# State-space stage of a hybrid trunk: the samples' state products in plain fp32 on four row groups, and the dense third bank in the shared four

## The chip, the cores and the metric

One Trainium2 chip, one core of it. The metric is the device time of one launch in microseconds (us). The kernel before takes 1957.69 us, the median of 3 runs (1957.03 to 1958.97).

## What is computed

One layer over two request groups with shared weights: a prompt of 1024 tokens and 8 samples of 16 tokens, 1152 tokens in all. Attention and a Mamba-2 state-space branch (SSD) are computed from one input projection and merged. What matters here is the state that the SSD branch leaves behind, cut from the reference:

```python
to_end = jnp.exp(a_cs[:, -1:] - a_cs)
h_new = h * jnp.exp(a_cs[:, -1])[..., None, None] + jnp.einsum('blgn,blgep->bgepn', bk, xdt * to_end[..., None])
```

For the samples the chunk is the sample's own 16 tokens, so the sum runs over 16 rows, for each of 8 samples, with B (`bk`, 16 x 128) on one side and the weighted x (16 x 128 for two heads) on the other. All 8 samples lie together on the 128 partitions, 16 rows each. TensorE contracts over partitions, so a product over one sample's 16 rows alone needs the other samples' rows set to zero, or left out.

## The kernel before

All dense projections are done in three fp32r products (L442, L443, L445: high weight by high x, high by low, low by high), accumulated in PSUM: for each block of 128 output channels three thirds of 384 tokens, each third 8 x 3 = 24 products. A third is here called a bank, since it fills one PSUM bank. The weights of a block are loaded as fp32 and split in two by ScalarE (L334, the high part) and VectorE (L335, the rest). Two blocks' split weights fit; the next pair of tiles is free only when the block before has finished its last product.

PSUM has eight banks: two for the dense banks (pool `d`, tiles of that name), two in one tile `s`, four shared ones in pool `g`, handed out in turn. In `dense` (L471) a block's first and second banks are `d`; the third, once attention is over, is the first half of an `s` tile.

The work beside the projections is written as generators. `run` steps the dense generator, and lets the others (urgent and paced ones) issue in between by a clock of estimated PE time (`yield 215`, `pause(1500)`). The tile framework then orders each engine's queue with its own timeline; that order is fixed in the program, and each engine executes its queue strictly in order. Some pieces are kept in program order (`late`).

The SSD stage goes over 16 pairs of heads p, in four groups of four pairs. For a group, `group_lat` (L1367) transposes B to token rows (L1384, copied out by ScalarE at L1385) and computes C times B (L1390, taken out by VectorE at L1392), all in `g` banks. For a pair, `prelude` (L1431) loads the decay rows `acs_d` by DMA (L1441), and ScalarE forms the decays from them (nine steps at L1453, an exponential at L1457; L1459 on VectorE multiplies by the masked C-B). The dense blocks of a pair are z (taken out by ScalarE at L1423, VectorE at L1424), the convolution's x (L1240, L1243, L1244 on ScalarE, then L1260 to L1270) and, for ten pairs, one merge gate (L1355, ScalarE). Then `main` (L1465): x is transposed (L1481) and weighted into `xd` and `xw` (L1485, VectorE), the chunk states are multiplied (L1526) and scanned (L1531, L1535), y is computed (L1553, L1560, both on column halves of the array; L1566), the carried states are added (L1573, L1578, L1579), and y is stored (L1588, L1590, L1591).

Last in a pair come the samples' states (L1594 to L1607). B and xw of the samples are split into a high and a low fp32r part, and laid out so that the 128 rows hold one half of the samples (64 rows) twice: high in one half of the partitions, low in the other (L1491 to L1508: ScalarE copies, VectorE differences). GpSimd makes four masked copies of x, `masked` (L1511), each for two samples of each half, with a mask of period four (`bmask4`). For each mask two products of 128 x 128 by 128 x 256 (B high, B low; L1598) are accumulated: four products in one `g` bank, twice per pair, with a pause between, and VectorE adds each bank to the state (L1607).

Of the kernel before, what the change touches and what calls it, by code (L numbers as in the profile page):

```python
# [7 lines left out]
F32 = mybir.dt.float32  # L8
# [4 lines left out]
P = 128  # L13
# [21 lines left out]
COLS = 53184  # L35
QCOLS = 1024
VCOLS = 6 * 1024
RCOLS = 16 * NT + 4 * 1024 + 1280 + 32
FCOLS = COLS - RCOLS - QCOLS - VCOLS
NQ = 3 * P  # L40

NQL = NQ + 32

C_ID, C_U, C_UB, C_ONE, C_BLK, C_BM, C_SEL, C_S4, C_BM4 = 0, 128, 256, 384, 512, 640, 648, 680, 712
NCONST = 716

PARAMS = [("norm_g", KT), ("b_ada", 24), ("conv_w", NCV * 4), ("conv_b", NCV), ("qk_g", 2), ("dskip", NPAIR),
          ("ssd_g", NPAIR), ("dt_bias", 32), ("a_log", 32)]
# [73 lines left out]
def trunk_kernel(ctx: ExitStack, tc: tile.TileContext, h):  # L122
# [55 lines left out]
    for n, w in PARAMS:  # L178
# [17 lines left out]
    bmask = cst[:, C_BM:C_BM + NB]  # L196
    sel = cst[:, C_SEL:C_SEL + 32]
    sel4 = cst[:, C_S4:C_S4 + 9]
    bmask4 = cst[:, C_BM4:C_BM4 + 4]

    H0 = 0
    W0 = H0 + 16 * NT
# [3 lines left out]
    L_ATT = arena.set_layout(Z0, [("Q", 1, 16 * P), ("T", 5, NT), ("S", 10, 640), ("U", 2, 640), ("K", 4, 512), ("q", 1, 256), ("d", 1, 256),  # L206
                                  ("k", 1, 128), ("p", 1, 128), ("n", 2, 36 + 3 * 16), ("t", 6, 14)])
    L_ATT["Z"] = L_ATT["T"][2:]
    L_SSD = arena.set_layout(Z0, [("X", 1, XW), ("R", 2, 1184), ("t", 8, 36), ("pad", 1, 576), ("T", 9, NT), ("Y", 1, 1184), ("H", 1, 1024),
                                  ("g", 3, G3)])  # L210
    L_HEAD = dict(L_SSD, T=[x for x in L_SSD["T"] if x[0] + x[1] <= Z0 + 7 * NT])
    L_START = arena.set_layout(Z0, [("T", 11, NT), ("ada", 5, 1024), ("e", 2, 256)])
    L_TAIL = arena.set_layout(Z0, [("T", 15, NT)])
# [4 lines left out]
    L_WA = rarena.set_layout(W0, [("w", 2, 1024)])  # L218
    L_QR = rarena.set_layout(W0 + 2 * 1024, [("q", 3, 1024)])
    L_Q = qarena.set_layout(0, [("q", 1, 1024)])  # L220
    L_ST = rarena.set_layout(W0 + 4 * 1024, [("b", 4, P), ("s", 2, P), ("x", 2, 2 * P)])
    L_W3 = varena.set_layout(0, [("w", 2, 3 * 1024)])
    L_W7 = varena.set_layout(0, [("w", 2, 7 * NQL)])
    L_QS = qarena.set_layout(0, [("ada", 1, 1024)])
# [4 lines left out]
    def alloc(lay, tag, cols, cold=None):  # L229
        if lay is L_Q:  # L230
            try:
                return alloc(L_QR, tag, cols)
            except NoSlot:
                pass
        if lay is L_SSD and tag == "H":
            try:
                return Buf(qarena, qarena.alloc(L_QS, "ada", cols), cols)
            except NoSlot:
                pass
        if lay is L_Q or lay is L_QS:  # L240
# [3 lines left out]
        if lay is L_H or lay is L_W or lay is L_WA or lay is L_QR or lay is L_ST:  # L244
# [182 lines left out]
    def dense(ops, evict, nk=KT, outs=1, last=False, wide=False, order=(0, 1, 2), other=False):  # L427

        i = widx[0]
        widx[0] += 1
        hi, lo = yield from w_wait(i)
        if len(jobs[min(i + 1, len(jobs) - 1)]) > 3:
            w_next(i)

        def mm(ps, o, g, k, parts=(0, 1)):
            tok = slice(g * G3, (g + 1) * G3)
            wc = slice((k * outs + o) * P, (k * outs + o + 1) * P)
            kh, kl = ops[k]  # L440
            if 0 in parts:
                nc.tensor.matmul(ps, hi.r[:, wc], kh.r[:, tok], start=k == 0, stop=False)  # L442
                nc.tensor.matmul(ps, hi.r[:, wc], kl.r[:, tok], start=False, stop=False)  # L443
            if 1 in parts:
                nc.tensor.matmul(ps, lo.r[:, wc], kh.r[:, tok], start=False, stop=k == nk - 1)  # L445

        for o in range(outs):
            if wide or (last and o == outs - 1):
                if wide or other:
                    acc = [pg(G3) for _ in range(3)]  # L450
                else:
                    sp = pss.tile([P, 2, 512], F32, tag="s", name=nm("s"))
                    acc = [psd.tile([P, G3], F32, tag="d", name=nm("d")) for _ in range(2)] + [sp[:, 0, :G3]]
                for k in range(nk):
                    while len(ops) <= k:
                        blocked[0] = "operand"
                        yield None
                    for g in range(3):
                        mm(acc[g], o, g, k)
                        if k == nk - 1:  # L460
                            yield from evict(o, g, slice(g * G3, (g + 1) * G3), acc[g]) or ()
                        yield 3 * 162.5
                    if last and o == outs - 1:
                        for x in ops[k]:
                            x.free()
                    if k == 2 and o == 0:
                        w_next(i)
                continue
            for g in order:
                if g == 2 and att_left[0] == 0:  # L470
                    ps = pss.tile([P, 2, 512], F32, tag="s", name=nm("s"))[:, 0, :G3]  # L471
                else:
                    ps = psd.tile([P, G3], F32, tag="d", name=nm("d"))
                for k in range(nk):
                    while len(ops) <= k:
                        blocked[0] = "operand"
                        yield None
                    mm(ps, o, g, k)
                    if nk == KT and g == order[-1] and k in (3, 5, 7):
                        w_over(i, k)  # L480
                    yield 3 * 162.5
# [880 lines left out]
    grp = {}  # L1362

    def group_dense(g, lay):
        res = grp[g] = {"b": [], "c": [], "sq": None, "st": None}
        yield from conv_gen(16 + g, lay, res["b"])
        yield from conv_gen(20 + g, lay, res["c"])  # L1367

# [31 lines left out]
    def ssd(p):  # L1400
# [62 lines left out]
        def main():  # L1463
# [24 lines left out]
            me, eb, h0, tm = st["me"]  # L1488
            ssd_all[p + 1] = True

            if res["st"] is None:  # L1491
                bs = res["st"] = []
                for j in range(2):
                    rw, ro = slice(64 * j, 64 * j + 64), slice(64 - 64 * j, 128 - 64 * j)
                    b_ = tokb.ap[rw, NP:]
                    hi = yield from walloc(L_ST, "b", P)
                    lo = yield from walloc(L_ST, "b", P)
                    nc.scalar.activation(hi.r[rw], b_, AF.Copy)
                    nc.scalar.activation(hi.r[ro], b_, AF.Copy)
                    nc.vector.tensor_tensor(lo.r[rw], b_, hi.ap[rw], ALU.subtract)  # L1500
                    nc.vector.tensor_tensor(lo.r[ro], b_, hi.ap[rw], ALU.subtract)
                    bs.append((hi, lo))
            xs = []
            for j in range(2):
                rw, ro = slice(64 * j, 64 * j + 64), slice(64 - 64 * j, 128 - 64 * j)
                t = yield from walloc(L_ST, "s", P)
                nc.scalar.activation(t.r[rw], xw.ap[rw, NP:], AF.Copy)
                nc.vector.tensor_tensor(t.r[ro], xw.ap[rw, NP:], t.ap[rw], ALU.subtract)  # L1508
                xs.append(t)

            def masked(q):  # L1511

                t = alloc(L_ST, "x", 2 * P)
                i = 2 * (q % 2)
                nc.gpsimd.tensor_tensor(t.r.rearrange("p (b n) -> p b n", n=P), xs[q // 2].ap.unsqueeze(1).to_broadcast([P, 2, P]),
                                        bmask4[:, i:i + 2].unsqueeze(2).to_broadcast([P, 2, P]), ALU.mult)
                return t

            xm = [masked(0), masked(1)]

            yield from pause(1500)
            for j in range(2):
# [68 lines left out]
            nc.scalar.activation(z.ap, x.ap, AF.Square)  # L1591
            stored(x)
            yield from pause(2000)
            pss_ = [pg(), pg()]  # L1594
            for q in range(4):
                j, i = q // 2, q % 2
                for w, b_ in enumerate(res["st"][j]):
                    nc.tensor.matmul(pss_[j][:, 2 * i * P:2 * (i + 1) * P], b_.r, xm[q].r, start=w == 0, stop=w == 1)  # L1598
                xm[q].free()
                if q < 2:  # L1600
                    xm.append(masked(q + 2))
                yield 215
                if q == 1:
                    yield from pause(4500)
                if i:
                    c = slice(4 * j * P, (4 * j + 4) * P)
                    nc.vector.tensor_tensor(h0.ap[:, c], h0.ap[:, c], pss_[j], ALU.add)  # L1607
            for t in xs + [xw]:
                t.free()
            if res["sq"] is None:  # L1610
                res["sq"] = z
            else:
# [4 lines left out]
            stored(h0)  # L1617
            if p % PPG == PPG - 1:
                s = res["sq"]
                for t in (tokb, res["cbm"], res["ct"], *res["st"][0], *res["st"][1]):  # L1620
# [304 lines left out]
```

## Time and profile before

| | |
|---|---|
| median of 3 runs | 1957.69 us |
| profiled execution, first to last instruction (span) | 1955.7 us |
| TensorE (PE) busy | 1938.3 us, 99% |
| VectorE (DVE) busy | 1168.5 us, 60% |
| ScalarE (ACT) busy | 776.4 us, 40% |
| GpSimd (POOL) busy | 323.5 us, 17% |
| granted TensorE clock | full in all 40 slices |

Of the profiled execution only the span is given; its time from outside isn't listed, so the span stands for it, 2.0 us under the median. A row of a timeline reads: start in us, length in us, engine, line, operation, output<-input, shape, number of instructions merged in the row, and in brackets the engine's idle time before it with what ended it. PE is TensorE's products, PEld its weight loads, SPq the queue that starts DMAs. A plain fp32 product appears as two records, an fp32r product as one. Attention runs until about 750 us, the SSD pairs from there to about 1520 us, the last projections after that.

### The profile page before, as it was taken

To read this page: it belongs to the slowest core of one execution; us is meant where nothing else is said; L and a number is where in the kernel's file an instruction comes from. 1 tells how busy PE (TensorE), PEld (TensorE's weight loads), DVE (VectorE), ACT (ScalarE), POOL (GpSimd) and SP (SyncE) were. 2 spreads that over 40 slices of the span, in tenths; PEclk is the share of its full clock that TensorE was granted. 3 is DMA by queue.
4 is the path that set the end of the run, shared out by engine and by line. 5 is a ranking of instruction groups with operands and counts; after the bars stand their busy time and mean duration, and the time that the engine had idled before them with its cause. 6 is when DMAs were issued, how large, how long until landed. Compare 5 with 4: busy or idle time off the path is not lost.

```text
span 1955.7 us, 35068 instructions
## 1 busy us (share of the span) xinstructions
PE 1938.3 (99%) x14091; PEld 1859.4 (95%) x14091; DVE 1168.5 (60%) x2441; ACT 776.4 (40%) x1589; POOL 323.5 (17%) x624
## 2 busy tenths in 40 slices
PE   7999999999999999999999999999999999999999
PEld 5999999899998999999999999999999999999999
DVE  7455555556555765757566666576674334777732
ACT  8444444445444557344454434345351301111200
POOL 0312213122131201212212221122212100000000
PEclk9999999999999999999999999999999999999999
DMA  9124244232432325433333333332337642331241
GB/s 367 60 81 131 86 132 131 90 122 88 131 112 96 112 88 160 128 112 110 95 132 129 106 103 114 117 118 91 117 118 291 234 140 92 104 104 56 86 143 52
DMA packets 81209, 238.62 MB, mean 122 GB/s; under 512 B 14284, under 2 KB 15320, under 8 KB 81048
## 3 DMA queue, kind: packets, MB, share of 16 engines
q1 hardware_dynamic: 72088, 207.74, 32.7%
q0 software_dynamic: 8960, 28.65, 3.8%
q8 instruction: 111, 1.82, 0.4%
q14 instruction: 50, 0.41, 0.1%
HBM read 192.70 MB, written 43.66 MB: 121 GB/s over the span
## 4 chain that ended last, share of the span: by engine, by line
PE 96%; DVE 1%; ACT 1%; DMA 1%; issue 0%; SPq 0%
PE d L442 13%; PE d L443 13%; PE d L445 13%; PE s L442 5%; PE s L445 5%; PE s L443 5%; PE d L508 5%; PE d L506 5%; PE d L507 5%; PE g L1043 3%; PE g L1066 3%; PE g L1553 2%; PE s L1122 2%; PE g L1526 1%; PE g L1573 1%; PE g L1122 1%
## 5 line engine op out<-in xcount | busy, mean ns | idle before, releaser
L442 PE MATMUL d<-rarena 128*128 128x384 f32 x1520 | 517.4, 340 | 0.3 <-ACT arena L1355 0.3
L445 PE MATMUL d<-rarena 128*128 128x384 f32 x1520 | 511.4, 336 | 0.0
L443 PE MATMUL d<-rarena 128*128 128x384 f32 x1520 | 511.0, 336 | 0.0
L442 PEld LDWEIGHTS d<-rarena 128*128 128x128 f32 x1520 | 285.6, 188 | 4.6 <-issue 2.3
L443 PEld LDWEIGHTS d<-rarena 128*128 128x128 f32 x1520 | 285.6, 188 | 2.8 <-issue 2.4
L445 PEld LDWEIGHTS d<-rarena 128*128 128x128 f32 x1520 | 285.5, 188 | 1.1 <-issue 0.9
L334 ACT ACTIVATE rarena<-arena 128x1024 fp32r<-128x1024 f32 x92 | 97.5, 1060 | 314.1 <-PE s L443 226.2
L442 PE MATMUL s<-rarena 128*128 128x384 f32 x640 | 216.7, 339 | 0.0
L443 PE MATMUL s<-rarena 128*128 128x384 f32 x640 | 214.2, 335 | 0.0
L445 PE MATMUL s<-rarena 128*128 128x384 f32 x640 | 214.1, 334 | 0.0
L508 PE MATMUL d<-va_att,rarena 128*128 128x384 f32 (+1 forms) x559 | 195.0, 349 | 0.0
L506 PE MATMUL d<-va_att,rarena 128*128 128x384 f32 (+1 forms) x559 | 193.9, 347 | 0.0
L507 PE MATMUL d<-va_att,rarena 128*128 128x384 f32 (+1 forms) x559 | 191.0, 342 | 0.0
L335 DVE TENSOR_TENSOR rarena<-arena,rarena 128x1024 fp32r<-128x1024 f32 x92 | 113.2, 1230 | 82.7 <-ACT rarena L334 82.4
L1031 ACT ACTIVATE arena<-arena 128x640 f32<-128x640 f32 (+2 forms) x144 | 101.4, 706 | 138.0 <-DVE arena L1140 99.7
L442 PEld LDWEIGHTS s<-rarena 128*128 128x128 f32 x640 | 120.3, 188 | 1.0 <-issue 1.0
L443 PEld LDWEIGHTS s<-rarena 128*128 128x128 f32 x640 | 120.3, 188 | 0.0
L445 PEld LDWEIGHTS s<-rarena 128*128 128x128 f32 x640 | 120.1, 188 | 0.0
L508 PEld LDWEIGHTS d<-va_att,rarena 128*128 128x128 f32 x559 | 105.5, 189 | 3.9 <-issue 2.7
L1263 DVE SCALAR_TENSOR_TENSOR arena<-arena 128x1176 f32<-128x1176 f32 x66 | 99.9, 1514 | 15.5 <-ACT arena L1260 14.2
L506 PEld LDWEIGHTS d<-va_att,rarena 128*128 128x128 f32 x559 | 105.2, 188 | 3.1 <-issue 1.2
L507 PEld LDWEIGHTS d<-va_att,rarena 128*128 128x128 f32 x559 | 105.2, 188 | 1.0 <-issue 0.4
(345 smaller groups left out, 3212.9 us busy)
## 6 DMA issues: line engine op xcount, KB each, us to landing
arena<-in_wall_dram SPq DMA_DIRECT2D x85, 512.0 KB, 3.9
arena<-in_kc_dram SPq DMA_DIRECT2D x64, 256.0 KB, 4.2
arena<-in_vc_dram SPq DMA_DIRECT2D x64, 256.0 KB, 3.4
arena<-acs_d SPq DMA_DIRECT2D x19, 576.0 KB, 3.8
gate_d<-arena POOLq DMA_DIRECT2D x48, 192.0 KB, 2.5
arena<-y_d SPq DMA_DIRECT2D x15, 576.0 KB, 5.6
arena<-in_wssd_dram SPq DMA_DIRECT2D x16, 512.0 KB, 4.1
arena<-in_wada_dram SPq DMA_DIRECT2D x15, 512.0 KB, 8.9
```

Of the source, the lines that this page charges most:

```text
L334: keep(nc.scalar.activation(hi.r[:, c], b.ap, AF.Copy))
L335: keep(nc.vector.tensor_tensor(lo.r[:, c], b.ap, hi.ap[:, c], ALU.subtract))
L442: nc.tensor.matmul(ps, hi.r[:, wc], kh.r[:, tok], start=k == 0, stop=False)
L443: nc.tensor.matmul(ps, hi.r[:, wc], kl.r[:, tok], start=False, stop=False)
L445: nc.tensor.matmul(ps, lo.r[:, wc], kh.r[:, tok], start=False, stop=k == nk - 1)
L506: nc.tensor.matmul(ps, kh.r[:, tok], wh, start=j == 0, stop=False)
L507: nc.tensor.matmul(ps, kh.r[:, tok], wl, start=False, stop=False)
L508: nc.tensor.matmul(ps, kl.r[:, tok], wh, start=False, stop=j == KT - 1)
L1031: nc.scalar.activation(p, p, AF.Exp, bias=sm_[:, 4 + e:5 + e], scale=-1.0, accum_out=sm_[:, 6 + e:7 + e])
L1043: nc.tensor.transpose(ps[:, s * P:(s + 1) * P], p[:, (j + s) * P:(j + s + 1) * P], ident)
L1122: late(nc.tensor.matmul(banks[k][e][:, o:o + w], x.r[hs, qs], y.r[hs, kk], start=i == 0, stop=i == 2))
L1263: nc.vector.scalar_tensor_tensor(yc, r.ap[:, j:j + n], w4[:, i, j:j + 1], yc, ALU.mult, ALU.add)
```

## The change

Three things are changed, and the SBUF layout that follows from them.

1. The samples' state products are plain fp32. No high and low parts are made any more. x of the samples (`xw`) is masked by parity: one GpSimd instruction per pair makes a tile of 2 x 128 columns, the left half with the even samples' rows kept, the right half with the odd ones (`parity`, a mask of period two). Rows 32r to 32r+32 hold samples 2r and 2r+1; so a product of these 32 rows of B with the same 32 rows of the tile gives both samples' states, 128 x 256. Four such products, one for each group of 32 rows, replace the eight.
2. Their outputs go to four banks: both halves of an `s` tile, and two `g` banks. VectorE adds the first two in one instruction, the others in one each.
3. A block's third dense bank is a `g` bank in place of the `s` tile, from the end of attention on.

```diff
@@ dense
                 if g == 2 and att_left[0] == 0:
-                    ps = pss.tile([P, 2, 512], F32, tag="s", name=nm("s"))[:, 0, :G3]
+                    ps = pg(G3)
@@ main of ssd(p)
-            if res["st"] is None:
...
-            for j in range(2):
-                rw, ro = slice(64 * j, 64 * j + 64), slice(64 - 64 * j, 128 - 64 * j)
-                t = yield from walloc(L_ST, "s", P)
-                nc.scalar.activation(t.r[rw], xw.ap[rw, NP:], AF.Copy)
-                nc.vector.tensor_tensor(t.r[ro], xw.ap[rw, NP:], t.ap[rw], ALU.subtract)
-                xs.append(t)
...
-            xm = [masked(0), masked(1)]
+            xm = yield from walloc(lay, "x", 2 * P)
+            nc.gpsimd.tensor_tensor(xm.ap.rearrange("p (b n) -> p b n", n=P), xw.ap[:, NP:].unsqueeze(1).to_broadcast([P, 2, P]),
+                                    parity.unsqueeze(2).to_broadcast([P, 2, P]), ALU.mult)
@@ end of main
-            pss_ = [pg(), pg()]
-            for q in range(4):
-                j, i = q // 2, q % 2
-                for w, b_ in enumerate(res["st"][j]):
-                    nc.tensor.matmul(pss_[j][:, 2 * i * P:2 * (i + 1) * P], b_.r, xm[q].r, start=w == 0, stop=w == 1)
...
-                yield 215
-                if q == 1:
-                    yield from pause(4500)
-                if i:
-                    c = slice(4 * j * P, (4 * j + 4) * P)
-                    nc.vector.tensor_tensor(h0.ap[:, c], h0.ap[:, c], pss_[j], ALU.add)
+            sp = pss.tile([P, 2, 512], F32, tag="s", name=nm("s"))[:, :, :2 * P]
+            pq = [sp[:, 0], sp[:, 1], pg(2 * P), pg(2 * P)]
+            for r in range(4):
+                rw = slice(32 * r, 32 * r + 32)
+                nc.tensor.matmul(pq[r], tokb.ap[rw, NP:], xm.ap[rw], start=True, stop=True)
+            xm.free()
+            yield 440
+            hp = h0.ap[:, :4 * P].rearrange("p (j c) -> p j c", c=2 * P)
+            nc.vector.tensor_tensor(hp, hp, sp, ALU.add)
+            for r in (2, 3):
+                c = slice(2 * r * P, 2 * (r + 1) * P)
+                nc.vector.tensor_tensor(h0.ap[:, c], h0.ap[:, c], pq[r], ALU.add)
```

In the changed kernel lines behind the cut have numbers lower by 26: L1481 and L1485 are the same, L1526 is L1500, L1535 is L1509, L1553 is L1527, L1566 is L1540, the new products are L1572.

The scheduler reorders the queues. First, TensorE's queue in the second pair. A name such as g611_8738 is a tile of pool `g` with its number, `rarena` the split weights and x, `va_ssd` and `arena` plain fp32 tiles. Before, four fp32r products stand between dense ones, and four more some thirty rows later:

```order
L442 MATMUL d610_8704<-rarena_70 128x384
L443 MATMUL d610_8704<-rarena_70 128x384
L445 MATMUL d610_8704<-rarena_70 128x384
L1598 MATMUL g611_8738<-rarena_70 128x256 x4
L442 MATMUL d610_8704<-rarena_70 128x384
```

Now the four new products, all together:

```order
L445 MATMUL d611_8682<-rarena_70 128x384
L1572 MATMUL s612_8720<-arena_69,va_ssd_7013 128x256 x2
L1572 MATMUL g613_8721<-arena_69,va_ssd_7013 128x256
L1572 MATMUL g614_8722<-arena_69,va_ssd_7013 128x256
L442 MATMUL d615_8736<-rarena_70 128x384
```

So it is in 15 of the 16 pairs; in the first pair two of them stand between L1527 and L1534, and the other two some 50 products later.

Second, TensorE's queue at the end of attention, where the first group's B is transposed (L1384) and multiplied with C (L1390). In brackets is the semaphore that an instruction waits for (DVE, Activation). `d573`, `d574` and `s575` are the three banks of the first merge gate; `s572`, now `g572`, is the third bank of the first pair's x. Before, `s572` was long done, and dense products of `d574` stand between the others:

```order
L1390 MATMUL g568_7888<-va_ssd_7013 128x128 [waits Activation_49]
L1390 MATMUL g568_7888<-va_ssd_7013 128x128 x3
L1384 MATMUL g569_7906<-arena_69,va_ssd_7013 128x128 [waits DVE_49]
L445 MATMUL d574_8019<-rarena_70 128x384
L442 MATMUL d574_8019<-rarena_70 128x384
L443 MATMUL d574_8019<-rarena_70 128x384
L445 MATMUL d574_8019<-rarena_70 128x384
L442 MATMUL d574_8019<-rarena_70 128x384
L443 MATMUL d574_8019<-rarena_70 128x384
L1390 MATMUL g570_7909<-va_ssd_7013 128x128 [waits DVE_49]
L445 MATMUL d574_8019<-rarena_70 128x384
```

Now `d573` and `d574` are done by this place, and the two third banks come behind the last product of C and B:

```order
L1390 MATMUL g568_7888<-va_ssd_7013 128x128 [waits DVE_49,PE_49]
L1390 MATMUL g568_7888<-va_ssd_7013 128x128 x3
L1384 MATMUL g569_7906<-arena_69,va_ssd_7013 128x128 [waits Activation_49]
L1390 MATMUL g570_7909<-va_ssd_7013 128x128 [waits DVE_49]
L442 MATMUL g572_7947<-rarena_70 128x384 [waits Activation_49]
L443 MATMUL g572_7947<-rarena_70 128x384
L445 MATMUL g572_7947<-rarena_70 128x384
```

Behind these stand the rest of `g572`'s 24 products, the 24 of `g575`, and then the next block's. The four shared banks are taken in turn: `g568`, `g569`, `g570` and `g572` follow `g567`, so `g572` takes the bank of `g567`, which ScalarE empties at L1385.

Third, ScalarE's queue at the same place. Before:

```order
L1385 ACTIVATE va_ssd_7013<-g564_7846 128x512
L1453 ACTIVATE arena_69<-arena_69 128x128 x9
L1385 ACTIVATE va_ssd_7013<-g567_7876 128x512
L1355 ACTIVATE arena_69<-d573_7977 128x384
L1453 ACTIVATE arena_69<-arena_69 128x128 x2
L1265 ACTIVATE arena_69<-arena_69 128x1176
L1453 ACTIVATE arena_69<-arena_69 128x128 x7
L1457 ACTIVATE arena_69<-arena_69 128x1152
L1385 ACTIVATE va_ssd_7013<-g569_7906 128x128
```

Now:

```order
L1385 ACTIVATE va_ssd_7013<-g564_7846 128x512
L1453 ACTIVATE arena_69<-arena_69 128x128 x9
L1385 ACTIVATE va_ssd_7013<-g567_7876 128x512
L1453 ACTIVATE arena_69<-arena_69 128x128 x7
L1355 ACTIVATE arena_69<-d574_8019 128x384
L1453 ACTIVATE arena_69<-arena_69 128x128 x2
L1385 ACTIVATE va_ssd_7013<-g569_7906 128x128
L1457 ACTIVATE arena_69<-arena_69 128x1152 x2
L1453 ACTIVATE va_ssd_7013<-va_ssd_7013,arena_69 128x128 x9
L334 ACTIVATE rarena_70<-arena_69 128x1024
```

The emptying of `g567` stands behind the nine L1453 as before; what has moved is that a dense bank now waits for it, that the weight split L334 for the block after `g575` stands behind all of these, and that x (L1260 to L1270) comes later: the first pair's transposes L1481 stand behind four more dense banks than before, and from them to L1534 no dense product is left between.

More of the change, by code (lines that the diff above doesn't have):

```diff
@@ L37 @@
 VCOLS = 6 * 1024
-RCOLS = 16 * NT + 4 * 1024 + 1280 + 32
+RCOLS = 16 * NT + 5 * 1024 + 32
 FCOLS = COLS - RCOLS - QCOLS - VCOLS
@@ L42 @@
 NQL = NQ + 32
-C_ID, C_U, C_UB, C_ONE, C_BLK, C_BM, C_SEL, C_S4, C_BM4 = 0, 128, 256, 384, 512, 640, 648, 680, 712
-NCONST = 716
+C_ID, C_U, C_UB, C_ONE, C_BLK, C_BM, C_SEL, C_S4, C_PAR = 0, 128, 256, 384, 512, 640, 648, 680, 712
+NCONST = 714
 PARAMS = [("norm_g", KT), ("b_ada", 24), ("conv_w", NCV * 4), ("conv_b", NCV), ("qk_g", 2), ("dskip", NPAIR),
@@ L198, in trunk_kernel @@
     sel4 = cst[:, C_S4:C_S4 + 9]
-    bmask4 = cst[:, C_BM4:C_BM4 + 4]
+    parity = cst[:, C_PAR:C_PAR + 2]
     H0 = 0
@@ L208, in trunk_kernel @@
     L_ATT["Z"] = L_ATT["T"][2:]
-    L_SSD = arena.set_layout(Z0, [("X", 1, XW), ("R", 2, 1184), ("t", 8, 36), ("pad", 1, 576), ("T", 9, NT), ("Y", 1, 1184), ("H", 1, 1024),
-                                  ("g", 3, G3)])
+    L_SSD = arena.set_layout(Z0, [("X", 1, XW), ("R", 2, 1184), ("t", 8, 36), ("x2", 1, 256), ("pad", 1, 320), ("T", 9, NT), ("Y", 1, 1184), ("H", 1, 1024),
+                                  ("g", 3, G3), ("x", 1, 256)])
+    L_SSD["x"] += L_SSD.pop("x2")
     L_HEAD = dict(L_SSD, T=[x for x in L_SSD["T"] if x[0] + x[1] <= Z0 + 7 * NT])
@@ L220, in trunk_kernel @@
     L_Q = qarena.set_layout(0, [("q", 1, 1024)])
-    L_ST = rarena.set_layout(W0 + 4 * 1024, [("b", 4, P), ("s", 2, P), ("x", 2, 2 * P)])
     L_W3 = varena.set_layout(0, [("w", 2, 3 * 1024)])
@@ L243, in alloc @@
             return Buf(varena, varena.alloc(lay, tag, cols), cols)
-        if lay is L_H or lay is L_W or lay is L_WA or lay is L_QR or lay is L_ST:
+        if lay is L_H or lay is L_W or lay is L_WA or lay is L_QR:
             return Buf(rarena, rarena.alloc(lay, tag, cols, cold), cols)
@@ L1364, in group_dense @@
     def group_dense(g, lay):
-        res = grp[g] = {"b": [], "c": [], "sq": None, "st": None}
+        res = grp[g] = {"b": [], "c": [], "sq": None}
         yield from conv_gen(16 + g, lay, res["b"])
@@ L1489, in main @@
             ssd_all[p + 1] = True
-            if res["st"] is None:
-                bs = res["st"] = []
-                for j in range(2):
-                    rw, ro = slice(64 * j, 64 * j + 64), slice(64 - 64 * j, 128 - 64 * j)
[L1495 to L1505, printed above, removed]
-                t = yield from walloc(L_ST, "s", P)
-                nc.scalar.activation(t.r[rw], xw.ap[rw, NP:], AF.Copy)
-                nc.vector.tensor_tensor(t.r[ro], xw.ap[rw, NP:], t.ap[rw], ALU.subtract)
-                xs.append(t)
[L1511 to L1517, printed above, removed]
-            xm = [masked(0), masked(1)]
+            xm = yield from walloc(lay, "x", 2 * P)
+            nc.gpsimd.tensor_tensor(xm.ap.rearrange("p (b n) -> p b n", n=P), xw.ap[:, NP:].unsqueeze(1).to_broadcast([P, 2, P]),
+                                    parity.unsqueeze(2).to_broadcast([P, 2, P]), ALU.mult)
             yield from pause(1500)
@@ L1593, in main @@
             yield from pause(2000)
-            pss_ = [pg(), pg()]
-            for q in range(4):
-                j, i = q // 2, q % 2
-                for w, b_ in enumerate(res["st"][j]):
[L1598 to L1601, printed above, removed]
-                yield 215
-                if q == 1:
-                    yield from pause(4500)
-                if i:
-                    c = slice(4 * j * P, (4 * j + 4) * P)
-                    nc.vector.tensor_tensor(h0.ap[:, c], h0.ap[:, c], pss_[j], ALU.add)
-            for t in xs + [xw]:
-                t.free()
+            sp = pss.tile([P, 2, 512], F32, tag="s", name=nm("s"))[:, :, :2 * P]
[10 more added lines that the diff above has]
+                nc.vector.tensor_tensor(h0.ap[:, c], h0.ap[:, c], pq[r], ALU.add)
+            xw.free()
             if res["sq"] is None:
@@ L1619, in main @@
                 s = res["sq"]
-                for t in (tokb, res["cbm"], res["ct"], *res["st"][0], *res["st"][1]):
+                for t in (tokb, res["cbm"], res["ct"]):
                     t.free()
@@ L1893 @@
     const[:, C_S4:C_S4 + 32] = (i[:, None] % 32) == np.arange(32)[None, :]
-    const[:, C_BM4:C_BM4 + 4] = (i[:, None] // NS) % 4 == np.arange(4)[None, :]
+    const[:, C_PAR:C_PAR + 2] = (i[:, None] // NS) % 2 == np.arange(2)[None, :]
     ar["const"] = const
```

## The prediction

> **What bounds the kernel now.** I read the page first: who is busy, and who is in the chain that ended last.
>
> ```profile
> PE 1938.3 (99%) x14091; PEld 1859.4 (95%) x14091; DVE 1168.5 (60%) x2441; ACT 776.4 (40%) x1589; POOL 323.5 (17%) x624
> PE 96%; DVE 1%; ACT 1%; DMA 1%; issue 0%; SPq 0%
> ```
>
> TensorE is busy for 99% of the span, and the chain runs through it for 96%. So work taken from ScalarE, VectorE or GpSimd is worth nothing by itself: 40, 60 and 17% busy. Only two things move the end: TensorE's own work, and time in which it waits. The view of waits, TensorE alone, shows how little it waits from the end of attention on:
>
> ```profile
> PE g L1481 <- DVE arena L1269: 1.8, 2, 1.4
> PE d L442 <- ACT arena L1355: 0.3, 1, 0.3
> ```
>
> 2.1 us in all, at the first two pairs. A new wait of TensorE is therefore paid in full, and the change is judged by two sums: the new products against the old, and the waits that the new order makes.
>
> **The change, part by part.**
>
> *The old products.* In the timeline, four of the eight stand between dense products:
>
> ```profile
> 783.44 0.33 PE L445 MATMUL d<-rarena 128*128 128x384 f32 x1
> 783.61 0.63 PE L1598 MATMUL g<-rarena 128*128 128x256 f32 x4
> 784.08 0.34 PE L442 MATMUL d<-rarena 128*128 128x384 f32 x1
> 784.26 0.34 PE L443 MATMUL d<-rarena 128*128 128x384 f32 x1
> ...
> 784.78 0.33 PE L443 MATMUL d<-rarena 128*128 128x384 f32 x1
> ```
>
> Lengths overlap, so I count from start to start. Three dense products take 784.78 - 784.26 = 0.52, 0.174 each. From the last dense start before to the second one behind are 784.26 - 783.44 = 0.82; less two dense steps, 0.47. Twice per pair: 0.95 us.
>
> *The new products.* Plain fp32 on groups of 32 rows isn't in this trace. The nearest row is plain fp32 on groups of 32 columns, 128 x 512, eight products in 16 records:
>
> ```profile
> 1571.17 0.34 PE L445 MATMUL s<-rarena 128*128 128x384 f32 x1
> 1571.44 0.62 PE L588 MATMUL g<-va_ssd,arena 128*32 128x512 f32 x2
> 1571.45 0.62 PE L588 MATMUL g<-arena 128*32 128x512 f32 x2
> 1571.89 0.60 PE L588 MATMUL g<-va_ssd,arena 128*32 128x512 f32 x2
> 1571.91 1.46 PE L588 MATMUL g<-arena 128*32 128x512 f32 x10
> 1573.29 0.44 PE L442 MATMUL d<-rarena 128*128 128x384 f32 x1
> 1573.57 0.34 PE L443 MATMUL d<-rarena 128*128 128x384 f32 x1
> ```
>
> The first records of four products start together (two rows at 1571.44 and 1571.45), their second records 0.44 later (1571.89): each product has two records, and the four groups run side by side. Four rounds, 1573.57 - 1571.17 - 0.35 = 2.05 us. A round without the first's start is 0.43, so 4 x 0.43 = 1.72 is streaming and 0.33 is the price of going into groups and back. For groups of rows there is a nearest row too, fp32r with two groups of 64 rows:
>
> ```profile
> 105.54 0.28 PE L1122 MATMUL g<-rarena 64*128 64x256 f32 x2
> 105.66 0.28 PE L1122 MATMUL g<-qa_att,rarena 64*128 64x256 f32 x2
> ```
>
> A row of two with the length of one (0.28) is two products of 256 columns that start together, and the next such row stands 0.12 later; the four in the old products' rows took 0.47, so 0.12 for one. Row groups overlap as column groups do. I take two rounds at half of 0.43, plus 0.33: 0.76 us for a pair's four products. A round on four banks of the same partitions at once is the unproven part; if the groups did not overlap at all it would be 4 x 0.43 + 0.33 = 2.05. By the Trainium skill ("TensorE: Matmul & The Clock Gate", Measured speedup vs the span model) four row groups of 32 gave 3.07 times, not four; by that the streaming would be an estimated 0.56 in place of 0.43, and the total below 2.1 us higher. No run here shows it yet.
>
> So 0.95 - 0.76 = 0.19 us less per pair, 15 pairs: -2.8 us. The first pair's products stand in two pieces, each with its own way in and out: 2 x 0.76 - 0.95 = +0.6. The new order also cuts the column-half products (L1553, now L1527) into two more pieces than before, at 0.33 each: +0.7. Sum of TensorE's own work: -1.5 us.
>
> *The third dense bank in the shared four.* This is where the waits change. The place is the end of attention. First TensorE, then the queue that starts DMAs, then ScalarE:
>
> ```profile
> 738.53 0.29 PE L1335 MATMUL g<-arena 128*32 128x128 f32 x1
> 750.14 0.38 PE L1390 MATMUL g<-va_ssd 128*128 128x128 f32 x2
> ```
>
> ```profile
> 743.56 0.83 SPq L1441 DMA_DIRECT2D arena<-acs_d  x2
> ```
>
> ```profile
> 744.53 0.60 ACT L1385 ACTIVATE va_ssd<-g 128x512 f32<-128x512 f32 x1 [2.79 <-PE g L1384]
> 748.63 2.74 ACT L1453 ACTIVATE arena<-arena 128x128 f32<-128x128 f32 x9 [3.50 <-DMA arena<-acs_d]
> 751.27 0.58 ACT L1385 ACTIVATE va_ssd<-g 128x512 f32<-128x512 f32 x1
> 751.75 0.47 ACT L1355 ACTIVATE arena<-d 128x384 f32<-128x384 f32 x1
> 752.12 0.69 ACT L1453 ACTIVATE arena<-arena 128x128 f32<-128x128 f32 x2
> ...
> 753.78 2.15 ACT L1453 ACTIVATE arena<-arena 128x128 f32<-128x128 f32 x7
> 755.83 1.15 ACT L1457 ACTIVATE arena<-arena 128x1152 f32<-128x1152 f32 x1
> 756.88 0.26 ACT L1385 ACTIVATE va_ssd<-g 128x128 f32<-128x128 f32 x1
> 757.04 0.48 ACT L1355 ACTIVATE arena<-d 128x384 f32<-128x384 f32 x1
> 757.41 1.17 ACT L1457 ACTIVATE arena<-arena 128x1152 f32<-128x1152 f32 x1
> 758.47 2.74 ACT L1453 ACTIVATE arena<-arena 128x128 f32<-128x128 f32 x9
> ```
>
> ScalarE stands idle until 748.63 for the DMA that spreads acs_d, and the second L1385 behind the nine L1453 ends at 751.85. Nobody minds: TensorE has dense work. In the new order `g572` needs the bank that this L1385 empties, and nothing dense is left ahead of it. When does TensorE get there? From L1335 to the last L1390 are 11.6 us, with 41 dense products between; now 27 are, so 14 x 0.174 = 2.4 less, and three fewer ahead of L1335, 0.5. It arrives at 750.5 - 2.9 = 747.6. L1385 starts from the same L1335 through the same DMA, so it ends 0.5 earlier, 751.35: TensorE waits 3.7 us. The queue has one DMA issue less ahead of the acs_d load, so the load may come up to 0.9 earlier: 2.8 to 3.9, I take 3.5.
>
> Behind the two third banks (48 x 0.174 = 8.4 us) comes the next block, whose weights ScalarE splits only after seven L1453 (2.15), L1355 (0.47), two L1453 (0.69), L1385 (0.26), two L1457 (1.15 and 1.17) and nine L1453 (2.74): 8.6 us. The page has the split itself:
>
> ```profile
> L334 ACT ACTIVATE rarena<-arena 128x1024 fp32r<-128x1024 f32 x92 | 97.5, 1060 | 314.1 <-PE s L443 226.2
> L335 DVE TENSOR_TENSOR rarena<-arena,rarena 128x1024 fp32r<-128x1024 f32 x92 | 113.2, 1230 | 82.7 <-ACT rarena L334 82.4
> ```
>
> The high part is there 8.6 + 1.06 = 9.7 us after L1385, 1.3 too late; four products go ahead without the low part (0.7), which comes 1.23 later: 0.5 more. 1.8 us, with bounds 0 (ScalarE packs tighter) and 2.5.
>
> Then the first pair's chain runs with no dense products in it:
>
> ```profile
> 759.89 2.87 DVE L1485 TENSOR_TENSOR arena<-g,arena 128x512 f32<-128x512 f32 x6
> 771.39 2.76 DVE L1535 SCALAR_TENSOR_TENSOR arena<-arena,g 128x64 f32<-128x64 f32 x14
> ```
>
> The second four state products (L1500) need the third of L1485's results, with one other VectorE instruction ahead; the dense bank behind L1534 needs a bank that the scan releases. By VectorE's 2.87 + 2.76 us and TensorE's own 7 us in this stretch I get 0.7 and 0.4: 1.1 us, bounds 0 and 2.
>
> New waits 3.5 + 1.8 + 1.1 = 6.4. The 2.1 us of old waits go, since x is ready long before the transposes get there. Net +4.3. In later pairs the order leaves over 3 us of TensorE's work between the release of a shared bank and its next use; I take 0 there, up to 1.
>
> *What is worth nothing.* The 48 ScalarE copies, 48 VectorE differences and 48 GpSimd maskings less are off the path. The new mask is one GpSimd instruction over 14 us ahead of its use (but for the first pair), the additions are behind everything that TensorE needs.
>
> *The sum.* -1.5 + 4.3 = +2.8 us on the span of 1955.7; the same on the median of 1957.69: 1960.5 us, 0.14% slower. About 0.2%, 3.9 us, is what a measurement of this kernel can tell from no change.
>
> **The rivals.**
>
> *Row groups in plain fp32 don't run four abreast.* The place is the products themselves: the second record of one product must follow its first in the same rows, and if the queue doesn't put the four first records ahead of the second ones, only a second record and the next product's first overlap. Then it is five rounds of 0.215 in place of two, +0.64 per pair, +10.3 in all: 1970.8; slower is decided already if 0.07 us more per pair is lost. Against it stand the L588 rows, where the order is four and four; for it, that those are columns, and that here a wait stands between the second and the third product. Chance 0.17. By the skill's 3.07 (same page and section as above) the time would be an estimated 1962.6.
>
> *The waits at the end of attention don't come.* If the DMA lands earlier, or TensorE's arrival is later than I count, the order costs nothing and the old 2.1 us go as well: -1.5 - 2.1 = -3.6, 1954.1. Against it: 3.50 us of idle time on that very DMA. Chance 0.15, half of it beyond 0.2%.
>
> *The change doesn't do what it says*: the products stand alone in 15 pairs by the order, so only their overlap is open, which is the first rival.
>
> **How the numbers follow.** The forecast's case has 0.68. Its new waits add up to 2.8 us with every lower bound and to 3.9 + 2.5 + 2 + 1 = 9.4 with every upper one; less the old 2.1 and less 1.5, that is -0.8 to +5.8, 1956.9 to 1963.5. About 0.3 of it lies beyond 0.2%. So: slower 0.21 + 0.17 = 0.38, faster 0.08, within 0.2% the rest, 0.54. The range runs from 1954.2, the second rival, to 1965.2, which adds to the forecast's upper end a first rival of 0.1 us per pair (1.7); that rival's full price is left out.
>
> **What would show it.** Right: L1572's first records starting together in fours, dense start to second dense start 1.1 us around them (0.76 plus two steps), a wait of 3 to 4 us of TensorE on L1385 near 748 us, and one on L334 and L335 some 9 us later. Wrong: the same stretch at 1.7 us or more, first records 0.2 apart, or TensorE passing 748 us without a gap. If further waits on shared banks show up in each pair, the price is theirs.

## The result, and the profile after

| | before | after |
|---|---|---|
| median (20 runs each) | 1957.45 us (1956.44 to 1960.29) | 1961.96 us (1958.67 to 1965.63) |
| ratio, 95% interval | | 1.0022 [1.0015, 1.0028] |
| profiled execution: span, its own time | 1955.7 us | 1962.9 us, 1964.68 us |

The changed kernel is 0.22% slower, 4.5 us by the medians. Its times are spread nearly twice as wide, and the profiled execution is the second longest of the 20: 7.2 us longer in span. The page of after, engines and chain:

```profile
PE 1941.3 (99%) x14091; PEld 1850.6 (94%) x14091; DVE 1154.9 (59%) x2409; ACT 761.1 (39%) x1541; POOL 280.3 (14%) x576
PE 94%; DMA 2%; ACT 1%; DVE 1%; issue 0%; SPq 0%; POOL 0%; DVEq 0%; POOLq 0%; ACTq 0%
```

TensorE still sets the time, but its share of the chain is 94% in place of 96%, and that of DMA 2% in place of 1%. The view of waits, TensorE alone (us in total, times, longest), without the rows of the start:

```profile
PE g L442 <- ACT va_ssd L1385: 2.3, 1, 2.3
PE d L442 <- ACT rarena L334: 1.9, 1, 1.9
PE g L1500 <- DVE arena L1485: 1.1, 3, 0.5
PE g L1481 <- DVE arena L1269: 1.0, 1, 1.0
...
PE d L445 <- DVE rarena L335: 0.3, 1, 0.3
```

6.6 us in place of 2.1: +4.5. The first is `g572` waiting for `g567`'s bank, the second and the last are the next block's weights. ScalarE in the timeline shows why both are late:

```profile
746.62 2.74 ACT L1453 ACTIVATE arena<-arena 128x128 f32<-128x128 f32 x9 [1.99 <-DMA arena<-acs_d]
749.26 0.57 ACT L1385 ACTIVATE va_ssd<-g 128x512 f32<-128x512 f32 x1
751.39 2.16 ACT L1453 ACTIVATE arena<-arena 128x128 f32<-128x128 f32 x7 [1.56 <-DMA arena<-acs_d]
...
756.68 2.74 ACT L1453 ACTIVATE va_ssd<-va_ssd,arena 128x128 f32<-128x128 f32 x9
759.31 1.06 ACT L334 ACTIVATE rarena<-arena 128x1024 fp32r<-128x1024 f32 x1
```

ScalarE stands for 1.99 and 1.56 us on the two loads of acs_d (one for each head), and L1385 and L334 are queued behind that work. Then comes something that the waits' view doesn't show, in TensorE's timeline:

```profile
760.42 0.44 PE L442 MATMUL d<-rarena 128*128 128x384 f32 x1 [1.94 <-ACT rarena L334]
...
761.68 0.67 PE L445 MATMUL d<-rarena 128*128 128x384 f32 x1 [0.28 <-DVE rarena L335]
762.14 0.53 PE L442 MATMUL d<-rarena 128*128 128x384 f32 x1
...
765.26 0.33 PE L443 MATMUL d<-rarena 128*128 128x384 f32 x1
```

Between 761.68 and 765.26 eleven dense products take 3.58 us, where 11 x 0.174 = 1.91 is normal: 1.7 us lost, though nothing is waited for. The view by stretches (first numbers: us busy of PE, PEld, DVE, ACT, POOL; then PEclk, DMA share, GB/s) has it in the granted clock. The stretches are laid by the trace's record of that clock: it changes at 14.21, 761.73 and 765.14 us, so the slow stretch lasts 3.41 us, and the 747.52 us between the first two are 219 times 3.413.

```profile
748.08:751.49 3.41, 1.60 (x9) 1.61 (x10) 0.08 (x1) 1.85 (x7) 0.00 (x0) 1.00 0.99 308
...
758.32:761.73 3.41, 1.19 (x6) 0.70 (x5) 1.30 (x2) 3.41 (x11) 1.03 (x2) 1.00 0.00 0
761.73:765.14 3.41, 3.41 (x11) 3.41 (x12) 0.63 (x1) 3.41 (x9) 0.63 (x2) 0.50 0.55 158
```

After a stretch of 3.41 us in which TensorE worked for 1.19, its clock is halved for the next 3.41 us. It is granted in full after the stretch at 748.08, in which TensorE worked for 1.60. So the waits cost more than their length.

Last, one set of the new products:

```profile
836.00 0.34 PE L445 MATMUL d<-rarena 128*128 128x384 f32 x1
836.27 0.48 PE L1572 MATMUL s<-arena,va_ssd 32*128 32x256 f32 x2
836.28 0.48 PE L1572 MATMUL g<-arena,va_ssd 32*128 32x256 f32 x2
836.59 0.38 PE L1572 MATMUL s<-arena,va_ssd 32*128 32x256 f32 x2
...
836.91 0.44 PE L442 MATMUL d<-rarena 128*128 128x384 f32 x1
837.20 0.34 PE L443 MATMUL d<-rarena 128*128 128x384 f32 x1
```

The four first records start within 0.02 us, the four second ones 0.32 later: all four run side by side. From dense start to second dense start are 837.20 - 836.00 = 1.20, less two steps 0.85 us; so it is in all 12 sets that stand between dense products.

### The profile page after: what moved, and what is told of

Same layout as the page of the kernel before. It is cut to its first block, busy times and chain, and to the rows that moved or that the text cites. A ratio compares the mean times of both kernels' runs of the same rounds, so it can differ in the third digit from the quotient of the medians.

```text
span 1962.9 us, 34912 instructions
## 1 busy us (share of the span) xinstructions
PE 1941.3 (99%) x14091; PEld 1850.6 (94%) x14091; DVE 1154.9 (59%) x2409; ACT 761.1 (39%) x1541; POOL 280.3 (14%) x576
## 4 chain that ended last, share of the span: by engine, by line
PE 94%; DMA 2%; ACT 1%; DVE 1%; issue 0%; SPq 0%; POOL 0%; DVEq 0%; POOLq 0%; ACTq 0%
PE d L442 13%; PE d L445 13%; PE d L443 13%; PE g L442 6%; PE g L443 6%; PE g L445 6%; PE d L508 5%; PE d L506 5%; PE d L507 5%; PE g L1043 3%; PE g L1066 3%; PE g L1527 2%; PE s L1122 2%; PE g L1500 1%; PE g L1547 1%; PE g L1122 1%
## 5 line engine op out<-in xcount | busy, mean ns | idle before, releaser
L442 PE MATMUL g<-rarena 128*128 128x384 f32 x752 | 253.3, 338 | 2.3 <-ACT va_ssd L1385 2.3
L443 PE MATMUL g<-rarena 128*128 128x384 f32 x752 | 251.7, 335 | 0.0
L445 PE MATMUL g<-rarena 128*128 128x384 f32 x752 | 251.1, 334 | 0.0
L334 ACT ACTIVATE rarena<-arena 128x1024 fp32r<-128x1024 f32 x92 | 97.4, 1059 | 316.1 <-PE g L443 258.9
L442 PEld LDWEIGHTS g<-rarena 128*128 128x128 f32 x752 | 141.2, 188 | 3.9 <-ACT va_ssd L1385 2.5
L443 PEld LDWEIGHTS g<-rarena 128*128 128x128 f32 x752 | 141.3, 188 | 0.0
L445 PEld LDWEIGHTS g<-rarena 128*128 128x128 f32 x752 | 141.1, 188 | 0.0
L1263 DVE SCALAR_TENSOR_TENSOR arena<-arena 128x1176 f32<-128x1176 f32 x66 | 95.4, 1446 | 8.6 <-ACT arena L1260 7.9
```

The lines of the kernel that those rows point to most:

```text
L334: keep(nc.scalar.activation(hi.r[:, c], b.ap, AF.Copy))
L1263: nc.vector.scalar_tensor_tensor(yc, r.ap[:, j:j + n], w4[:, i, j:j + 1], yc, ALU.mult, ALU.add)
```

## The experiments

The first theory (A): the loss is made at the end of attention by the third bank, as waits and the slow clock that follows them. The rival (B): the sets of plain fp32 products, with the way in and out, cost it. Ratios are to the kernel before, run beside each on the same chip.

**The third bank alone**, with the old products:

```diff
@@ dense (the kernel before)
-                    ps = pss.tile([P, 2, 512], F32, tag="s", name=nm("s"))[:, 0, :G3]
+                    ps = pg(G3)
```

> The old products with only the third dense bank moved to the shared four. Theory A (the loss is made at the end of attention, by the third bank): the same three waits as in the changed kernel, about 2.3 us on L1385, 1.9 on L334 and 0.6 on L335, followed by some 3 us at half the granted clock (1.6 us lost); 4.5 + 1.6 above the kernel before, 1963.5 us (1961.5 to 1965). Rival B (the lone rounds of plain fp32 products and what stands around them cost the time, the third bank is neutral): 1957 to 1958 us.

Measured: 1964.21 us, ratio 1.0033 [1.0021, 1.0046]. The order at the end of attention is that of the changed kernel, and so is the loss; the waits:

```profile
PE g L442 <- ACT va_ssd L1385: 5.9, 1, 5.9
...
PE d L445 <- DVE rarena L335: 0.3, 1, 0.3
```

Here the acs_d load came late, so that one wait of 5.9 us took the place of two; behind it stand 13 dense steps of 0.32 us in place of 0.174. A holds, B falls: the third bank makes the loss without any new product. That the wait on L334 went is what A had wrong: ScalarE has the same work to do in either case, so what TensorE waits longer for L1385 it doesn't wait for the weights.

**The products alone**, the third bank back in the `s` tile:

```diff
@@ dense (the changed kernel)
-                    ps = pg(G3)
+                    ps = pss.tile([P, 2, 512], F32, tag="s", name=nm("s"))[:, 0, :G3]
```

> The new products with the third dense bank left in the s tile. The order cuts the four products into two and two in 13 pairs, because the s tile is in use. Theory A: no wait of 1 us of TensorE on L1385 or L334; full clock throughout; but a piece of two costs as much as one of four (0.83 beside 0.85 us), so 29 pieces x 0.84 - 32 x 0.475 = +9 us: 1966 us (1964 to 1968). If a piece of two cost half of one of four: 26 x 0.42 + 3 x 0.85 - 15.2 = -1.7, 1956 us. Rival B: 1961 us or more, with the end of attention the same as before.

Measured: 1964.94 us, ratio 1.0037 [1.0023, 1.0050]. No wait on L1385 or L334, full clock, and still 7.8 us slower. A piece of two, in TensorE's timeline:

```profile
825.97 0.34 PE L445 MATMUL d<-rarena 128*128 128x384 f32 x1
826.24 0.70 PE L1572 MATMUL g<-arena,va_ssd 32*128 32x256 f32 x4
826.87 0.44 PE L442 MATMUL d<-rarena 128*128 128x384 f32 x1
827.15 0.34 PE L443 MATMUL d<-rarena 128*128 128x384 f32 x1
```

827.15 - 825.97 - 0.35 = 0.83 us for two, as much as for four. So the move of the third bank isn't a separate idea: the new products are worth nothing unless the `s` tile is free for them. Here B has a point: sets that are torn apart do cost.

**The third bank in the shared four only from the second pair on:**

```diff
@@ dense (the changed kernel)
-                    ps = pg(G3)
+                    ps = pg(G3) if ssd_all[2] else pss.tile([P, 2, 512], F32, tag="s", name=nm("s"))[:, 0, :G3]
```

> The changed kernel, but the third bank stays in the s tile until the second pair's main part has begun, and is in the shared four from then on. The order at the end of attention is the one of before, and all 16 sets of four products stand together. Theory A: the old waits (about 2 us) and no others, full clock; 16 x 0.85 - 32 x 0.475 = -1.6, and one more piece of L1527 (+0.3): 1956.2 us (1955 to 1957.5), below both kernels. Rival B: 1961 us or more, as the changed kernel.

Measured: 1954.84 us, ratio 0.9989 [0.9980, 0.9997], below both kernels. From the end of attention on TensorE waits in one row only:

```profile
PE g L1481 <- DVE arena L1269: 1.2, 2, 1.1
```

The same products as in the changed kernel, but 2.3 us below the kernel before beside it, in place of 4.5 above: where the third bank stands in the first pair decides the sign. (The order that follows from it also keeps the first pair's four products in one piece, which the changed kernel pays for with about 0.6 us.)

**L1385 on VectorE:**

```diff
@@ group_lat (the changed kernel)
-            nc.scalar.activation(tok.ap[:, c], pt[:, :n * P], AF.Copy)
+            nc.vector.tensor_copy(tok.ap[:, c], pt[:, :n * P])
```

> The changed kernel with the copy of the transposed B (L1385) on VectorE in place of ScalarE; TensorE's order at the end of attention is unchanged. The bank of g572 is then free before TensorE gets there, and ScalarE, with 1.4 us of copies less and the weight split L334 ahead of nine L1453 (2.7 us), has the next weights about 4 us earlier. Theory A: the waits on L1385 and L334 shrink to 0 to 0.7 together, the clock stays full, 4.1 + 1.6 less: 1956.5 us (1955.5 to 1959). Rival C (only the wait moves: VectorE or another late weight takes its place): still 2 us or more of waits between 745 and 765 us, 1960 to 1962 us. Rival B: 1961 to 1962 us.

Measured: 1960.14 us, ratio 1.0017 [1.0008, 1.0025]. The wait for the bank is gone, that for the weights isn't. First the waits, then ScalarE in the timeline:

```profile
PE d L442 <- ACT rarena L334: 1.4, 1, 1.4
...
PE d L445 <- DVE rarena L335: 0.8, 1, 0.8
```

```profile
747.42 2.74 ACT L1453 ACTIVATE arena<-arena 128x128 f32<-128x128 f32 x9 [7.32 <-DMA arena<-acs_d]
...
755.53 1.04 ACT L334 ACTIVATE rarena<-arena 128x1024 fp32r<-128x1024 f32 x1
```

C is right and A's number wrong: with the bank free TensorE reaches the weights at 755.2, and L334, still behind the acs_d load, ends at 756.6. TensorE is busy for 1.17 of the 3.41 us from 755.19, and ten steps of 0.32 us follow. Taking one waiter off a late producer hands the wait to the next.

**One more round of products**, and **all four on the same rows**:

```diff
@@ end of main (the changed kernel)
-            for r in range(4):
+            for r in (0, 1, 2, 3, 0, 1, 2, 3):
@@ end of main (the changed kernel; the other one)
-                nc.tensor.matmul(pq[r], tokb.ap[rw, NP:], xm.ap[rw], start=True, stop=True)
+                nc.tensor.matmul(pq[r], tokb.ap[0:32, NP:], xm.ap[0:32], start=True, stop=True)
```

> The changed kernel with the four state products issued twice in a row into the same banks (the second four write the same values again): 15 sets of eight. It prices one more round. In the changed kernel a set of four takes 0.85 us from dense to dense. Theory F (what was underestimated is a fixed price of a lone set, for going into row groups and back; a further round streams at 2 x 256 columns, 0.215): 1.06 us for a set of eight. Theory W (every round pays 0.33 from its first to its second records, for its weights): 1.50 us. Rival (groups overlap only in the first round): 1.7 us or more. A single time, 1965 to 1972 us, says little; the set is read from the profile.

> The changed kernel with all four state products on the first 32 rows (it leaves out the states of the samples in the other 96 rows). Same number of products, banks and columns, only the row groups coincide. Theory (separate row groups are what lets the four run side by side): first records no longer 7 ns apart; records one behind the other, 8 x 0.11 us and more for a set, 1.4 us if the weights are hidden and up to 3.1 if each product pays 0.33 between its records. Rival (four banks alone allow the overlap): 0.85 us, as in the changed kernel.

The timeline of the first (one time: 1970.39 us), then of the second (1982.92 us):

```profile
834.15 0.34 PE L445 MATMUL d<-rarena 128*128 128x384 f32 x1
834.42 0.48 PE L1572 MATMUL s<-arena,va_ssd 32*128 32x256 f32 x2
...
834.74 0.38 PE L1572 MATMUL s<-arena,va_ssd 32*128 32x256 f32 x2
...
834.95 0.38 PE L1572 MATMUL s<-arena,va_ssd 32*128 32x256 f32 x2
...
835.17 0.38 PE L1572 MATMUL s<-arena,va_ssd 32*128 32x256 f32 x2
...
835.77 0.34 PE L443 MATMUL d<-rarena 128*128 128x384 f32 x1
```

```profile
836.11 0.34 PE L445 MATMUL d<-rarena 128*128 128x384 f32 x1
836.38 1.13 PE L1572 MATMUL s<-arena,va_ssd 32*128 32x256 f32 x4
837.35 1.02 PE L1572 MATMUL g<-arena,va_ssd 32*128 32x256 f32 x4
838.30 0.44 PE L442 MATMUL d<-rarena 128*128 128x384 f32 x1
838.58 0.34 PE L443 MATMUL d<-rarena 128*128 128x384 f32 x1
```

Eight take 835.77 - 834.15 - 0.35 = 1.27: the second round adds 0.42, two records of 0.21. Neither F nor W had that number (F had counted a record of 256 columns at half its length). On the same rows four take 838.58 - 836.11 - 0.35 = 2.12, three more products adding 1.27, 0.42 each. So four products on four row groups stream in the time of one, and a set of 0.85 is 0.43 of streaming and 0.42 of going in and out.

**The waits filled with work**, to see what the clock follows. In these two kernels the dense lines are L449 to L452.

```diff
@@ the changed kernel
+    def fill(ops, n):
+        fp = pss.tile([P, 2, 512], F32, tag="s", name=nm("s"))
+        for z in range(n):
+            late(nc.tensor.matmul(fp[:, 0, :G3], ops[0][0].r[:, :P], ops[z % KT][1].r[:, :G3], start=True, stop=True))
@@ dense: ahead of the first pair's third bank; ahead of the block after the second third bank (first kernel only)
+                        fill(ops, 13)
+                    fill(ops, 12)
```

> The changed kernel with 25 extra fp32r products of 128 x 384 into the idle s tile, read by nobody: 13 ahead of the first pair's third bank, 12 between the second third bank and the next block, 0.174 us each, 4.35 us of work put where TensorE waits for L1385 and L334. Theory G (a stretch of some 3.4 us in which TensorE is idle for about two thirds halves its clock for the next 3.4 us): the work hides in the waits, no dense step of 0.32 us is left unless the acs_d load lands very late, and the 1.6 us of slow clock go: 1960.3 us (1958.5 to 1962). Rival H (the slow clock has nothing to do with TensorE's idle time): the slow steps stay, 1961.5 to 1963. Rival I (the waits are shorter in most executions than in the profiled one, so the extra work isn't hidden): 1963 us or more.

Measured: 1965.09 us, ratio 1.0035 [1.0023, 1.0047], which is rival I's time. But by the profile both fillings hide in the waits: the second runs from 759.38 to 761.46 us, while ScalarE's L334 ends only at 761.07, and at the end of attention a wait of 1.4 us on the copy of L1385 is left, at full clock. The order behind has changed too: a wait of 2.2 us on L1485's results in the second pair is new. The stretches before and behind its end:

```profile
814.10:817.50 3.40, 1.19 (x9) 0.90 (x8) 3.19 (x5) 1.87 (x4) 0.00 (x0) 1.00 0.16 58
817.50:820.90 3.40, 3.40 (x19) 3.07 (x20) 3.40 (x9) 0.28 (x1) 1.14 (x2) 0.50 0.17 59
```

So the slow clock is there too, at another place and behind another wait, after a stretch in which TensorE worked for 1.19 of 3.4 us: G's condition. Its price can't be read from a kernel that lost the clock elsewhere, and what else makes the 1965.09 us wasn't taken apart. So the first filling was tried alone, beside the changed kernel:

> The changed kernel with the first filling alone: 13 extra fp32r products (2.26 us, read by nobody) ahead of the first pair's third bank; the order of everything behind is that of the changed kernel. Theory G (TensorE idle for some 2.2 us or more of a 3.4 us stretch gets half its clock for the next 3.4 us): the idle time on L1385 shrinks by 2.26 us, below 2.2 unless acs_d lands very late, and where it does no 0.32 us steps follow; the kernel is 1 to 1.6 us faster than the changed one in spite of 2.26 us more work, 1960.5 us beside 1962. Rival H (the slow clock has other causes): slow steps as before, the same time as the changed kernel, or more. Rival I (the extra work isn't hidden): 1 to 2.3 us slower than the changed kernel.

> The changed kernel on the same chip and in the same rounds as the run with 13 extra products, so that the two can be compared: 1962 us (1959 to 1965). Its profile is one more sample of the wait: after 4.5 us or more of waits between 745 and 765 us, or 2.2 us within 3.4, slow steps of 0.32 us.

Measured: 1962.83 us (ratio 1.0031 [1.0019, 1.0043]) with the 13 products, 1962.47 us (1.0026 [1.0016, 1.0036]) without. In the filled kernel's profile the wait on L1385 is down to 0.3 us; the longest is 1.4 us on L334. The stretches around that one, laid by this profile's own clock record (its change at 11.61 us lies 219 x 3.413 before 759.13):

```profile
759.13:762.54 3.41, 2.24 (x11) 1.92 (x12) 1.23 (x1) 3.41 (x9) 1.65 (x3) 1.00 0.11 20
762.54:765.95 3.41, 3.41 (x22) 3.41 (x21) 2.86 (x3) 3.41 (x5) 0.54 (x1) 1.00 0.53 181
```

And the unfilled one beside it, first its longest wait, then its stretches:

```profile
PE g L442 <- ACT va_ssd L1385: 3.7, 1, 3.7
```

```profile
747.20:750.60 3.40, 0.00 (x0) 0.00 (x0) 0.47 (x2) 3.10 (x10) 0.00 (x0) 1.00 1.04 279
750.60:754.00 3.40, 3.24 (x10) 3.24 (x11) 0.00 (x0) 3.40 (x13) 0.54 (x1) 0.50 0.71 240
```

2.26 us of work cost 0.4 us of median. The intervals are too wide to rule out rival I's 1 to 2.3 us by the times alone, but in the profile the work stands where TensorE waited. Idle for a third of a stretch, the filled kernel keeps its clock; idle for all of it, the unfilled one loses half. That agrees with G's condition, and so do the mean clocks of the single runs, given to three places (one stretch at half the clock takes 0.0009 off): four of the six filled runs kept 1.000, and one of the eight unfilled ones. G's price, 1 to 1.6 us off the median, did not show: the four filled runs with their clock took 1960.62 to 1963.98 us. How the work added and the clock saved offset each other stays open.

**The changed kernel once more**, for its spread:

> The changed kernel, unaltered, for a second profile. Theory: its times are spread over 7 us because the load of acs_d lands at another time in each execution, and with it the wait on L1385 (0 to 6 us) and whether the clock is halved behind it; the sets of four are the same 0.847 us to 0.005, so the spread is not theirs. The span should be 1955.7 + 1 (the rest) + the waits' sum less 2.1 + 1.6 if there are slow steps, within 1 us. Rival: the sets or the later pairs differ between executions by 0.1 us a pair.

Measured: one time, 1963.25 us. The sets are 0.847 us again, and the span is 1961.4 us, where the expected sum gives 1955.7 + 1 + 6.1 - 2.1 + 1.6 = 1962.3. The longest wait, and the stretches before and in the slow clock:

```profile
PE g L442 <- ACT va_ssd L1385: 4.8, 1, 4.8
```

```profile
748.40:751.80 3.40, 0.00 (x0) 0.00 (x0) 0.00 (x0) 2.84 (x10) 0.00 (x0) 0.99 1.00 271
751.80:755.20 3.40, 2.97 (x9) 2.97 (x10) 0.00 (x0) 3.40 (x12) 0.31 (x1) 0.51 0.78 224
```

L1385 and the weights together: 4.5, 4.8 and 3.7 us in the three profiles of the changed kernel. The wait moves about with the landing of acs_d, while the sets stay the same. That is enough for part of the spread; how much of the 7 us it makes three profiles don't tell. The 20 runs of the result fit it: the six with a mean clock of 1.000 have a median of 1960.4 us, the 14 with less 1962.5. But a long wait brings both the lost time and the lost clock, so this doesn't part them.

## Why the prediction was right, and where its terms were off

The forecast was 1960.5 us, 0.14% slower; measured 1961.96, 0.22%. The mechanism that sets the sign, the wait of a dense bank for a copy behind acs_d, was the one that was named. The closeness is in part luck: against the profile of after the sum was 4.9 us short (7.7 - 2.8), in terms that all erred to the same side: 0.2 for the waits, 1.3 for the sets, 1.7 for the rest that the fourth point below takes up, 1.7 for the clock. That execution is one of the longest, and the median lies nearer.

- *The waits at the end of attention.* Net +4.3 forecast, 6.6 - 2.1 = +4.5 in the profile of after. Its parts shifted: 3.5 for the bank was 2.3, 4.8 and 3.7; 1.8 for the weights was 2.2, 0 and 0. The forecast saw the chain of ScalarE behind acs_d rightly, but took the load's landing as fixed, and its start as at most 0.9 us earlier; it was issued 2.85 us earlier (740.71 in place of 743.56). It also had no second stop on acs_d, the 1.56 us ahead of the seven L1453.
- *The first pair without dense products.* 1.1 forecast; L1500 waited for 0.7 of its 1.1 us there. "Later pairs 0, up to 1" was 1.4 in the profile: 1.0 at L1481 of a later pair, 0.4 at L1500 of the second.
- *The sets.* 0.76 us forecast, 0.85 measured in the 12 that can be priced between dense products; for 15 that is -1.5 in place of -2.8. The streaming was right (0.43), the fixed price mis-sized, 0.42 in place of 0.33: that came from a row of column groups with several rounds behind each other. The first pair's two pieces, +0.6, fit: its second piece took 0.83.
- *Other products in more pieces.* +0.7 forecast for L1527. From TensorE's first product to its last the profile of after is 7.7 us longer; 7.7 - 4.5 - 1.7 + 1.5 - 0.6 = 2.4 is left. About 1 us of it, an estimate, belongs to the waits. The view counts a wait from the end of the record before, 0.17 us behind the place where the next step would have begun: from 758.15, the last dense start before the wait on L334, to 760.42 are 2.27 us, which less a step of 0.174 is 2.10, where the view has 1.94. The step behind takes 0.28 in place of 0.174. After has seven such waits and before three. The order has L1527 in 22 pieces in place of 19, which at the forecast's 0.33 makes 1.0 in place of 0.7. L1481 is in 20 pieces in place of 17, but so it is with the third bank moved later, where the same sum leaves 0.5 (2.05 us shorter from first product to last, of which 0.9 are waits and 1.6 the 16 sets). No run took the rest apart. So TensorE's own work, forecast at -1.5, saved nothing in the end.
- *What the forecast lacked.* The halved clock behind the waits, 1.7 us in the profile of after.
- *The rivals.* "Don't run four abreast" falls by the records of the sets and by the same-rows run. "The waits don't come" falls by all three profiles. By the Trainium skill ("TensorE: Matmul & The Clock Gate", Measured speedup vs the span model) four row groups gave 3.07 times; here the streaming of four takes 0.42 to 0.43 us and of one 0.42, four times, and the measured figure holds. A whole set with its way in and out is 2.12 / 0.85 = 2.5 times faster than on one group.

Where the gain went, then: the products save 1.5 us less what the first pair and the torn pieces take back, and a bank that moved for their sake puts a late DMA on TensorE's path in the first pair, for 4.5 us and a slow clock. The starts of the dense products show where: the 1153rd of the 6840 starts at 824.58 us before and 832.01 after, 7.4 us later, and the last one 7.6 us later. The sets of 15 pairs lie in between, and their 1.5 us are lost again on the way, to a wait of 1.0 us on L1269 among others; with the third bank moved later 0.6 us of them are left.

## What to carry to other kernels

Before a buffer is moved to a shared pool, look up who empties the bank that it will inherit, and what that engine is waiting for: here a copy behind a DMA that nobody minded. A wait taken from one consumer of a late producer goes to the next one, so move the consumer's place in the order instead, at the one spot where it matters. Price small products by the set, way in and out included, since two cost as much as four.

## What the runs showed of the hardware that was not expected

- *The clock falls after less than a whole idle stretch.* In stretches laid by each profile's clock record, TensorE was busy for 1.19 of 3.41 us (after), 1.17 (L1385 on VectorE) and 1.19 (both fillings): half clock in the next 3.41 us. Busy for 1.60 (after) and 2.24 (13 products): full clock. So in these profiles the border lies between 35% and 47% of a stretch. The Trainium skill ("TensorE: Matmul & The Clock Gate", What's actually happening) gives half clock after an idle window of about 3.4 us, in a free-running window. The length and the free running agree with the clock record (14.21, 761.73, 765.14 us in after); but two gaps of 1.94 and 0.28 us were enough, none of them a whole window, and the measurement decides. Every profile with 3.7 us or more of idle time in one piece at the end of attention had slow steps, seven to thirteen of 0.32 us.
- *The same load lands at very different times.* acs_d, issued at 740.1 to 740.7, let ScalarE start at 746.62 (after), 747.42 (L1385 on VectorE), 748.96 (after again) and 749.90 (third bank alone), with a DMA share of 0.98 to 1.06 in the view by stretches between 745 and 751.8 us in three of them.
- *A piece of two products on row groups costs what four cost,* 0.83 beside 0.85 us.
